# Latent attention: P times V as native fp32 matmuls instead of three fp32r matmuls on high and low parts

## The chip, the cores and the metric

The kernel runs on one core of one Trainium2 chip. A core has a matrix engine (TensorE, PE in the profile, with its weight loads shown as PEld), VectorE (DVE), ScalarE (ACT), GpSimd (POOL) and SyncE (SP), on whose queue nearly all of this kernel's DMAs are issued. The engines run their own instruction streams in order and meet at semaphores. The metric is the device time of one execution in microseconds; the times given are medians of several runs.

## The reference, cut to what matters

The kernel computes two layers of a diffusion backbone: 1024 latent tokens and 256 context tokens of width 1024. Layer 0 holds differential attention with 4 heads: each head has two query/key maps of width 64 and one value of width 128. Latent queries read all 1280 keys, context queries only the 256 context keys. Everything is in fp32.

```python
def diff_attend(q, k, v, lam):
    s = jnp.einsum('bhmqd,bhmkd->bhmqk', q, k).astype(jnp.float32) * (DA_HEAD_DIM ** -0.5)
    p = jax.nn.softmax(s, axis=-1)
    p = p[:, :, 0] - lam * p[:, :, 1]
    return jnp.einsum('bhqk,bhkv->bhqv', p.astype(v.dtype), v)
```

The last line is the product of this document. Behind it come an RMS norm over the 128 values of a head, the output projection, and a gated ConvFFN; layer 1 has pooling and retention in place of convolution and attention, and another FFN.

## The kernel before

**High and low parts.** Most matrix products are made of three fp32r matmuls: each operand x is split into a high part h, its copy in fp32r, and a low part l = x - h, and the product is h*h + h*l + l*h, accumulated in PSUM (`mm3`, lines 215 to 219). ScalarE writes the high part, VectorE subtracts for the low one. A few products, the retention in layer 1 among them (lines 1133, 1153, 1167, 1168), are given fp32 operands directly, as native fp32 matmuls.

**The stages.** Layer 0 projects all tokens, then computes the gates of the convolution, with the attention of the context tokens (`att_ctx`, line 592) and the streamed modulation matrix woven in (some 250 to 430 us of the span). Then `attention` (line 1252) weaves two generators, step by step in proportion: the context tokens' output projection and FFN (`chain`), and the attention of the latent tokens (`att_lat`, line 629). From about 860 us the latent tokens' output projection and FFN follow, then layer 1.

**A head.** `att_head` (line 658) loads K of both maps and V of one head by DMA on SP's queue. All three loads go through one buffer, `kraw`. K is cast by ScalarE and its lower half subtracted on VectorE; V is split into `vh` (line 675, ScalarE) and `vl` (line 677, VectorE), with two buffers each in the latent stage and one each in the context stage.

**A block.** `AttBlock` (line 1438) handles 512 latent queries of one head (256 for the context), as four tiles of 128 queries. For each tile, `scores` makes both maps' scores in PSUM (lines 1470 and 1471), takes the maximum on VectorE (1472) and the exponential on ScalarE (1474); there is one PSUM buffer for scores, three banks wide, so the second map waits for the first one's exponential. `combine` (line 1487, VectorE) adds the two maps with their factors. `product` transposes the combined P tile by tile of 128 keys on TensorE, four to a PSUM tile `tpp` (line 1504), copies each to `pth` (1505, ScalarE) and subtracts for `ptl` (1506, VectorE). Two query tiles share one `pth`/`ptl` pair of 256 columns; after the second one, `product` runs `mm3` for each of ten key tiles (two for the context): thirty matmuls with V as the stationary operand, into `pv`. ScalarE reads `pv` twice (1514, 1515); `stats` and `out` finish the norm and write to DRAM. There are 16 such groups of ten key tiles in the latent stage, and 4 of two in the context stage.

PSUM holds two `w` buffers, which `tpp`, `pv` and the norm's small tiles take in turn, next to the scores and three buffers of the chain. The weights of all matrix products come through one stream that runs two units ahead.

Of the kernel before, what the change touches and what calls it, by code (L numbers as in the profile page):

```python
# [9 lines left out]
F32 = mybir.dt.float32  # L10
F32R = mybir.dt.float32r
AF = mybir.ActivationFunctionType
ALU = mybir.AluOpType
# [4 lines left out]
P = 128  # L18
# [44 lines left out]
class Pool:  # L63


    def __init__(self, pool, tags):
        self.pool, self.tags = pool, tags
# [17 lines left out]
def weave(*gens):  # L85

    live = [[g, n, 0] for g, n in gens]
    while live:
        e = min(live, key=lambda e: (e[2] + 0.5) / e[1])
        if next(e[0], StopIteration) is StopIteration:  # L90
            live.remove(e)
        e[2] += 1
# [44 lines left out]
class Net:  # L137
# [454 lines left out]
    def att_ctx(self, gp, ps):  # L592

        self.att_small(gp)
        yield
        pp = Pool(ps, {"S": ("st", 1), "w": ("tp", 2)})
        ap = Pool(gp, {t: (t, 1) for t in ("kraw", "k0", "k1", "vh", "vl", "qraw", "qa0", "qa1", "qb0", "qb1", "s1", "osq",
                                          "osb", "p0", "p1", "pth", "ptl", "e1", "r1")})
        for h in range(4):
            head = self.att_head(ap, h, SEQ, CTX)  # L600
            b = AttBlock(self, ap, pp, h, SEQ, CTX, head, SEQ, CTX)
            yield
            for qt in range(2):
                b.scores(qt)
                b.combine(qt)
                yield
                b.product(qt)
                yield
            b.stats()
            yield  # L610
            b.out()
# [46 lines left out]
    def att_head(self, ap, h, t0, N):  # L658

        nc = self.nc  # L660
        K = []
        n = N // P
        for m in range(2):
            raw = ap.tile([P, N], F32, tag="kraw", name="kraw")
            for d in range(2):
                nc.sync.dma_start(raw[d * 64:(d + 1) * 64, :], self.kT[m * 64:(m + 1) * 64, h, t0:t0 + N])
            kt = ap.tile([P, N], F32R, tag=f"k{m}", name=f"k{m}")
            nc.scalar.copy(kt, raw)
            nc.vector.tensor_tensor(kt[64:128, :], raw[64:128, :], kt.bitcast(F32)[64:128, :], op=ALU.subtract)
            K.append(kt)  # L670
        raw = ap.tile([P, N], F32, tag="kraw", name="vraw")
        nc.sync.dma_start(raw.rearrange("p (t v) -> p t v", t=n),
                          self.vD[t0:t0 + N, h * P:(h + 1) * P].rearrange("(t p) v -> p t v", p=P))
        vh = ap.tile([P, N], F32R, tag="vh", name="vh")
        nc.scalar.copy(vh, raw)
        vl = ap.tile([P, N], F32R, tag="vl", name="vl")
        nc.vector.tensor_tensor(vl, raw, vh.bitcast(F32), op=ALU.subtract)
        return K, vh, vl


    def out_proj(self, xk, T, o, v, src, alloc, tmp, ps, gate):
# [570 lines left out]
    def attention(self):  # L1252

        nc, tc, I = self.nc, self.tc, self.I
        B = self.modB
        with ExitStack() as s:
            cp = s.enter_context(tc.tile_pool(name="cp", bufs=1, reuse_waits="tile"))
            ap = s.enter_context(tc.tile_pool(name="ap", bufs=1, reuse_waits="tile"))
            pp = s.enter_context(tc.tile_pool(name="psS", bufs=1, space=PSUM, reuse_waits="tile"))
            xc = cp.tile([P, 8, CTX], F32, name="xc")  # L1260
            xk = lambda k: xc[:, k, :]
            s4c = lambda: cp.tile([P, 2, CTX], F32R, tag="s4c", name="s4c", bufs=14)
            tmp = self.tmp
            ps = Pool(pp, {"mm": ("mm", 3), "tp": ("mm", 3), "st": ("mm", 3)})

            def chain():
                op = self.out_proj(xk, CTX, SEQ, 1, self.mix, s4c, tmp, ps, lambda m, v: B[:, m, v:v + 1])
                next(op)
                nc.sync.dma_start(xc, I["ctxT"])
                yield  # L1270
                yield from op
                hs = []
                yield from self.norm(xk, CTX, self.gs[(0, 2, 1)], lambda k: B[:, 8 + k, 1:2], s4c, tmp, ps, hs, True)
                big = Pool(cp, {"a": ("a", 2), "b": ("b", 1), "cv": ("cv", 2), "e": ("e", 1)})
                yield from self.ffn(0, xk, CTX, hs, 4, s4c, big, ps, lambda m: B[:, 24 + m, 1:2])
                nc.sync.dma_start(self.xcD, xc)

            at = Pool(ap, {t: (t, 2) for t in ("k0", "k1", "vh", "vl", "qa0", "qa1", "qb0", "qb1", "s1", "p0", "p1",
                                               "e1", "r1")})
            pw = Pool(pp, {"w": ("w", 2), "S": ("S", 1)})  # L1280
            ch = chain()
            for _ in range(11):
                next(ch)
            weave((ch, 9 + 2 + 22 + 6 * 4 - 11), (self.att_lat(at, pw), 68))
# [153 lines left out]
class AttBlock:  # L1438


    def __init__(self, net, ap, pp, h, q0, Q, head, k0, nk):
        nc = net.nc
        self.net, self.nc, self.ap, self.pp, self.h, self.q0, self.Q = net, nc, ap, pp, h, q0, Q
        self.K, self.vh, self.vl = head
        self.nk = nk
        self.q = []
        for m in range(2):
            raw = ap.tile([P, Q], F32, tag="qraw", name="qraw")
            for d in range(2):
                nc.sync.dma_start(raw[d * 64:(d + 1) * 64, :], net.qT[m * 64:(m + 1) * 64, h, q0:q0 + Q])  # L1450
            a = ap.tile([P, Q], F32R, tag=f"qa{m}", name=f"qa{m}")
            nc.scalar.copy(a, raw)
            b = ap.tile([P, Q], F32R, tag=f"qb{m}", name=f"qb{m}")
            nc.vector.tensor_tensor(b, raw, a.bitcast(F32), op=ALU.subtract)
            self.q.append((a, b))
        self.s1 = ap.tile([P, 4], F32, tag="s1", name="s1")
        self.sq = net.tmp.tile([P, 512], F32, tag="t2k", name="osq")[:, :Q]
        self.o = net.tmp.tile([P, 512], F32, tag="t2k", name="osb")[:, :Q]
        self.st = {}
# [32 lines left out]
    def product(self, qt):  # L1492
        nc, ap, net = self.nc, self.ap, self.net
        nkt = self.nk // P
        p = self.st.pop(qt)[0][0]
        if qt % 2 == 0:
            self.pt = [ap.tile([P, nkt, 256], F32R, tag=t, name=t) for t in ("pth", "ptl")]
        pth, ptl = self.pt
        cs = slice((qt % 2) * P, (qt % 2 + 1) * P)
        for k0 in range(0, nkt, 4):  # L1500
            n = min(4, nkt - k0)
            tp = self.pp.tile([P, 4, P], F32, tag="w", name="tpp")
            for j in range(n):
                nc.tensor.transpose(tp[:, j, :], p[:, (k0 + j) * P:(k0 + j + 1) * P], net.ident)
            nc.scalar.copy(pth[:, k0:k0 + n, cs], tp[:, :n, :])
            nc.vector.tensor_tensor(ptl[:, k0:k0 + n, cs], tp[:, :n, :], pth.bitcast(F32)[:, k0:k0 + n, cs],
                                    op=ALU.subtract)
        if qt % 2 == 1:
            pv = self.pp.tile([P, 512], F32, tag="w", name="pv")[:, :256]
            for kt in range(nkt):  # L1510
                vs = slice(kt * P, (kt + 1) * P)
                net.mm3(pv, (self.vh[:, vs], self.vl[:, vs]), (pth[:, kt, :], ptl[:, kt, :]), kt == 0, kt == nkt - 1)
            os = slice((qt - 1) * P, (qt + 1) * P)
            nc.scalar.activation(self.sq[:, os], pv, AF.Square)
            nc.scalar.mul(self.o[:, os], pv, net.subg)
# [136 lines left out]
```

## Time and profile before

| | us |
|---|---|
| median of 3 runs | 2654.31 |
| lowest, highest | 2648.61, 2654.50 |
| the profiled execution | 2658.96 |
| its span | 2657.2 |
| TensorE busy, matmuls | 2551.8 (96%) |
| TensorE busy, weight loads | 2145.4 (81%) |
| VectorE busy | 1947.5 (73%) |
| ScalarE busy | 1166.3 (44%) |
| mean granted clock of TensorE | 0.974 |

The span is what the trace covers, from the first instruction to the end of the last; the execution's time holds a little around it. Busy time is the union of an engine's instructions. Matmuls are pipelined: each record lasts longer than the time to the next one's start, so TensorE can be busy in this sense and still have room; the distance from start to start tells its pace. The granted clock is 1.00 at 2.4 GHz and 0.50 at 1.2 GHz. A tile of the program stands in a row as out<-in, with its line; "128x256" is partitions by elements.

### The profile page before, as it was taken

To read this page: it belongs to the slowest core of one execution; us is meant where nothing else is said; L and a number is where in the kernel's file an instruction comes from. 1 tells how busy PE (TensorE), PEld (TensorE's weight loads), DVE (VectorE), ACT (ScalarE), POOL (GpSimd) and SP (SyncE) were. 2 spreads that over 40 slices of the span, in tenths; PEclk is the share of its full clock that TensorE was granted. 3 is DMA by queue.
4 is the path that set the end of the run, shared out by engine and by line. 5 is a ranking of instruction groups with operands and counts; after the bars stand their busy time and mean duration, and the time that the engine had idled before them with its cause. 6 is when DMAs were issued, how large, how long until landed. Compare 5 with 4: busy or idle time off the path is not lost.

```text
span 2657.2 us, 34664 instructions
## 1 busy us (share of the span) xinstructions
PE 2551.8 (96%) x12666; PEld 2145.4 (81%) x12666; DVE 1947.5 (73%) x3077; ACT 1166.3 (44%) x1751; POOL 241.4 (9%) x321
## 2 busy tenths in 40 slices
PE   6999998999998998999999998999899999999999
PEld 6777887999997886888888886877688788888887
DVE  7467965999997587777778978446558766666984
ACT  5322324767675354444443454133235444444442
POOL 3221000000000041000000002013203100000000
PEclk6999999999999999999999999999799999999999
DMA  7224545443433624434458664577662222225874
GB/s 257 93 95 135 182 135 165 134 143 112 124 116 111 232 65 149 134 127 133 130 178 302 218 206 141 177 232 222 191 217 72 103 88 80 87 80 202 281 242 139
DMA packets 209547, 414.01 MB, mean 156 GB/s; under 512 B 20320, under 2 KB 89568, under 8 KB 208992
## 3 DMA queue, kind: packets, MB, share of 16 engines
q1 hardware_dynamic: 206352, 406.41, 46.6%
q10 hardware_dynamic: 3024, 5.38, 0.6%
q8 instruction: 99, 1.62, 0.3%
q14 instruction: 72, 0.59, 0.1%
HBM read 341.98 MB, written 69.73 MB: 155 GB/s over the span
## 4 chain that ended last, share of the span: by engine, by line
PE 63%; DVE 13%; issue 12%; DMA 7%; ACT 3%; POOL 2%; SPq 0%; ACTq 0%; DVEq 0%; POOLq 0%
PE PA L217 4%; PE PA L218 4%; PE PA L219 4%; PE pd L218 3%; PE pd L219 3%; PE pd L217 3%; PE PB L217 2%; PE PB L218 2%; PE PB L219 2%; PE pt L217 2%; PE pt L218 2%; PE pt L219 2%; PE po L218 2%; PE po L217 2%; PE po L219 2%
## 5 line engine op out<-in xcount | busy, mean ns | idle before, releaser
L114 DVE TENSOR_TENSOR wl<-wr,wh 128x1024 fp32r<-128x1024 f32 x254 | 309.6, 1221 | 178.4 <-ACT wh L112 176.1
L112 ACT CAST wh<-wr 128x1024 fp32r<-128x1024 f32 x254 | 261.9, 1034 | 394.1 <-PE PA L218 67.3
L217 PE MATMUL pd<-s,wh 128*128 128x512 f32 x616 | 241.2, 392 | 4.9 <-ACT s L963 4.9
L218 PE MATMUL pd<-s,wh 128*128 128x512 f32 x616 | 241.4, 392 | 1.8 <-DVE s L964 1.8
L219 PE MATMUL pd<-s,wl 128*128 128x512 f32 x616 | 241.1, 391 | 0.0
L217 PE MATMUL PA<-s,wh 128*128 128x512 f32 x544 | 212.2, 390 | 0.2 <-DVE a L893 0.2
L219 PE MATMUL PA<-s,wl 128*128 128x512 f32 x544 | 211.8, 389 | 0.0
L218 PE MATMUL PA<-s,wh 128*128 128x512 f32 x544 | 211.8, 389 | 0.0
L351 DVE SCALAR_TENSOR_TENSOR mw<-mw,cr 128x256 f32<-128x256 f32 x256 | 111.4, 458 | 81.3 <-DMA mw<-in_mod1T 71.9
L112 ACT CAST wh<-r 128x1024 fp32r<-128x1024 f32 x80 | 67.0, 837 | 220.6 <-PE PB L218 126.5
L217 PEld LDWEIGHTS pd<-s,wh 128*128 128x128 f32 x616 | 116.4, 189 | 29.4 <-ACT s L963 5.3
L218 PEld LDWEIGHTS pd<-s,wh 128*128 128x128 f32 x616 | 116.4, 189 | 27.2 <-DVE s L964 3.2
L219 PEld LDWEIGHTS pd<-s,wl 128*128 128x128 f32 x616 | 116.4, 189 | 24.2
L217 PE MATMUL PB<-s,wh 128*128 128x512 f32 x320 | 125.0, 390 | 1.2 <-ACT p L889 1.2
L218 PE MATMUL PB<-s,wh 128*128 128x512 f32 x320 | 124.8, 390 | 0.0
L219 PE MATMUL PB<-s,wl 128*128 128x512 f32 x320 | 124.6, 389 | 0.0
L217 PEld LDWEIGHTS PA<-s,wh 128*128 128x128 f32 x544 | 102.2, 188 | 22.3 <-DVE a L893 1.3
L219 PEld LDWEIGHTS PA<-s,wl 128*128 128x128 f32 x544 | 102.1, 188 | 21.2
L218 PEld LDWEIGHTS PA<-s,wh 128*128 128x128 f32 x544 | 102.2, 188 | 21.1
L1474 ACT ACTIVATE p<-S,s 128x1280 f32<-128x1280 f32 (+1 forms) x80 | 92.9, 1161 | 52.7 <-DVE s L1472 51.2
L359 POOL TENSOR_TENSOR rr<-vv,mhalf 128x8 f32<-128x8 f32 (+2 forms) x39 | 57.6, 1478 | 587.8 <-DVE vv L357 563.3
L1472 DVE TENSOR_REDUCE s<-S 128x1 f32<-128x1280 f32 (+1 forms) x80 | 102.0, 1275 | 11.1 <-PE S L1471 10.1
(385 smaller groups left out, 7000.3 us busy)
## 6 DMA issues: line engine op xcount, KB each, us to landing
wr<-in_w_up SPq DMA_DIRECT2D x98, 512.0 KB, 3.4
wr<-in_w_dn SPq DMA_DIRECT2D x92, 512.0 KB, 4.3
gr<-gD SPq DMA_DIRECT2D x154, 256.0 KB, 3.7
mw<-in_mod1T SPq DMA_DIRECT2D x256, 128.0 KB, 3.2
gD<-fcv SPq DMA_DIRECT2D x44, 512.0 KB, 3.6
wr<-in_w_out SPq DMA_DIRECT2D x40, 512.0 KB, 4.2
r<-in_w_up SPq DMA_DIRECT2D x40, 512.0 KB, 3.3
mbw<-in_mod0T SPq DMA_DIRECT2D x32, 512.0 KB, 3.6
```

Of the source, the lines that this page charges most:

```text
L112: self.nc.scalar.copy(hi, raw)
L114: eng.tensor_tensor(lo, raw, hi.bitcast(F32), op=ALU.subtract)
L217: mm(out, L[0], R[0], start=first, stop=False)
L218: mm(out, L[0], R[1], start=False, stop=False)
L219: self.last_mm = mm(out, L[1], R[0], start=False, stop=last)
L351: self.nc.vector.scalar_tensor_tensor(w, in0=w, scalar=1.0, in1=c, op0=ALU.mult, op1=ALU.mult, accum_out=d)
L359: self.last_pow = nc.gpsimd.tensor_tensor(r, vv, self.mhalf[:, :n], op=ALU.pow)
L1472: nc.vector.tensor_reduce(s2[:, m:m + 1], sv, axis=AX.X, op=ALU.max, negate=True)
L1474: nc.scalar.activation(e, sv, AF.Exp, bias=s2[:, m:m + 1], accum_out=self.s1[:, qt:qt + 1] if m == 0 else s2[:, 2:3])
```

## The change

`product` writes the transposed P once, as fp32, into `pt`, and multiplies it with V as it came from DRAM, one native fp32 matmul per key tile. The high copies and low subtractions of P and V go, V gets a buffer of its own in place of `kraw` (two in the latent stage, one in the context stage), and `pt` has two buffers in the latent stage where `pth` and `ptl` had one each. Scores, softmax and everything else stay. The product's arithmetic becomes that of the fp32 matmul instead of the three-term sum.

```diff
@@ -594,8 +594,8 @@
         self.att_small(gp)
         yield
         pp = Pool(ps, {"S": ("st", 1), "w": ("tp", 2)})
-        ap = Pool(gp, {t: (t, 1) for t in ("kraw", "k0", "k1", "vh", "vl", "qraw", "qa0", "qa1", "qb0", "qb1", "s1", "osq",
-                                          "osb", "p0", "p1", "pth", "ptl", "e1", "r1")})
+        ap = Pool(gp, {t: (t, 1) for t in ("kraw", "k0", "k1", "vh", "qraw", "qa0", "qa1", "qb0", "qb1", "s1", "osq",
+                                          "osb", "p0", "p1", "pt", "e1", "r1")})
         for h in range(4):
             head = self.att_head(ap, h, SEQ, CTX)
             b = AttBlock(self, ap, pp, h, SEQ, CTX, head, SEQ, CTX)
@@ -668,14 +668,10 @@
             nc.scalar.copy(kt, raw)
             nc.vector.tensor_tensor(kt[64:128, :], raw[64:128, :], kt.bitcast(F32)[64:128, :], op=ALU.subtract)
             K.append(kt)
-        raw = ap.tile([P, N], F32, tag="kraw", name="vraw")
-        nc.sync.dma_start(raw.rearrange("p (t v) -> p t v", t=n),
+        V = ap.tile([P, N], F32, tag="vh", name="V")
+        nc.sync.dma_start(V.rearrange("p (t v) -> p t v", t=n),
                           self.vD[t0:t0 + N, h * P:(h + 1) * P].rearrange("(t p) v -> p t v", p=P))
-        vh = ap.tile([P, N], F32R, tag="vh", name="vh")
-        nc.scalar.copy(vh, raw)
-        vl = ap.tile([P, N], F32R, tag="vl", name="vl")
-        nc.vector.tensor_tensor(vl, raw, vh.bitcast(F32), op=ALU.subtract)
-        return K, vh, vl
+        return K, V
 
 
     def out_proj(self, xk, T, o, v, src, alloc, tmp, ps, gate):
@@ -1275,7 +1271,7 @@
                 yield from self.ffn(0, xk, CTX, hs, 4, s4c, big, ps, lambda m: B[:, 24 + m, 1:2])
                 nc.sync.dma_start(self.xcD, xc)
 
-            at = Pool(ap, {t: (t, 2) for t in ("k0", "k1", "vh", "vl", "qa0", "qa1", "qb0", "qb1", "s1", "p0", "p1",
+            at = Pool(ap, {t: (t, 2) for t in ("k0", "k1", "vh", "pt", "qa0", "qa1", "qb0", "qb1", "s1", "p0", "p1",
                                                "e1", "r1")})
             pw = Pool(pp, {"w": ("w", 2), "S": ("S", 1)})
             ch = chain()
@@ -1441,7 +1437,7 @@
     def __init__(self, net, ap, pp, h, q0, Q, head, k0, nk):
         nc = net.nc
         self.net, self.nc, self.ap, self.pp, self.h, self.q0, self.Q = net, nc, ap, pp, h, q0, Q
-        self.K, self.vh, self.vl = head
+        self.K, self.V = head
         self.nk = nk
         self.q = []
         for m in range(2):
@@ -1494,22 +1490,20 @@
         nkt = self.nk // P
         p = self.st.pop(qt)[0][0]
         if qt % 2 == 0:
-            self.pt = [ap.tile([P, nkt, 256], F32R, tag=t, name=t) for t in ("pth", "ptl")]
-        pth, ptl = self.pt
+            self.pt = ap.tile([P, nkt, 256], F32, tag="pt", name="pT")
+        pt = self.pt
         cs = slice((qt % 2) * P, (qt % 2 + 1) * P)
         for k0 in range(0, nkt, 4):
             n = min(4, nkt - k0)
             tp = self.pp.tile([P, 4, P], F32, tag="w", name="tpp")
             for j in range(n):
                 nc.tensor.transpose(tp[:, j, :], p[:, (k0 + j) * P:(k0 + j + 1) * P], net.ident)
-            nc.scalar.copy(pth[:, k0:k0 + n, cs], tp[:, :n, :])
-            nc.vector.tensor_tensor(ptl[:, k0:k0 + n, cs], tp[:, :n, :], pth.bitcast(F32)[:, k0:k0 + n, cs],
-                                    op=ALU.subtract)
+            nc.scalar.copy(pt[:, k0:k0 + n, cs], tp[:, :n, :])
         if qt % 2 == 1:
             pv = self.pp.tile([P, 512], F32, tag="w", name="pv")[:, :256]
             for kt in range(nkt):
                 vs = slice(kt * P, (kt + 1) * P)
-                net.mm3(pv, (self.vh[:, vs], self.vl[:, vs]), (pth[:, kt, :], ptl[:, kt, :]), kt == 0, kt == nkt - 1)
+                net.last_mm = nc.tensor.matmul(pv, self.V[:, vs], pt[:, kt, :], start=kt == 0, stop=kt == nkt - 1)
             os = slice((qt - 1) * P, (qt + 1) * P)
             nc.scalar.activation(self.sq[:, os], pv, AF.Square)
             nc.scalar.mul(self.o[:, os], pv, net.subg)
```

## Rows read from the trace of the kernel before

**Rows 1.** Stretch, length; busy PE, PEld, DVE, ACT, POOL; clock; DMA share, GB/s.

```profile
480.00:825.00 345.00, 340.30 (x2607) 323.70 (x2605) 325.56 (x475) 241.04 (x417) 15.08 (x47) 1.00 0.40 123
822.00:860.00 38.00, 27.58 (x181) 24.96 (x180) 27.05 (x45) 18.82 (x34) 1.01 (x1) 0.90 0.32 112
```

**Rows 2.** Timeline of TensorE in latent attention (start, length, instruction).

```profile
506.99 0.28 PE L217 MATMUL pv<-pth,vh 128*128 128x256 f32 x1
...
510.41 0.39 PE L1471 MATMUL S<-k,qb 128*128 128x512 f32 x1
510.64 0.28 PE L1470 MATMUL S<-k,qa 128*128 128x256 f32 x1
...
510.87 0.28 PE L219 MATMUL pab<-s4c,wl 128*128 128x256 f32 x1
...
511.94 0.28 PE L219 MATMUL pab<-s4c,wl 128*128 128x256 f32 x1
...
841.27 1.03 PE L1504 MATMUL tpp<-ident,p 128*128 128x128 f32 x8
```

**Rows 3.** TensorE's instructions by form, 480 to 825 (busy, mean ns, idle).

```profile
L219 PE MATMUL pab<-s4c,wl 128*128 128x256 f32 x327 | 93.9, 287 | 0.0
...
L1470 PE MATMUL S<-k,qa 128*128 128x512 f32 x115 | 48.4, 421 | 1.8 <-ACT p L1474 1.4
...
L217 PE MATMUL pd<-s4c,wh 128*128 128x256 f32 x163 | 46.8, 288 | 0.0
...
L1504 PE MATMUL tpp<-ident,p 128*128 128x128 f32 x288 | 42.6, 274 | 1.0 <-DVE osb L1533 0.5 <-DVE ptl L1506 0.4
...
L217 PE MATMUL pv<-pth,vh 128*128 128x256 f32 x140 | 39.4, 281 | 0.1
```

**Rows 4.** Timeline of all engines at the start of latent attention.

```profile
459.36 0.63 PE L375 MATMUL rb<-ident,rr 128*128 128x128 f32 x2
...
460.38 1.49 DVE L677 TENSOR_TENSOR vl<-vraw,vh 128x1280 fp32r<-128x1280 f32 x1 [2.11 <-ACT vh L675]
...
461.79 0.47 DVE L402 SCALAR_TENSOR_TENSOR nt<-xc,gs,rb 128x256 f32<-128x256 f32 x1
```

**Rows 5.** What TensorE waited for, 822 to 860 us (total us, times, longest).

```profile
PE S L1470 <- ACT p L1474: 3.7, 2, 2.8
PE tpp L1504 <- DVE p L1487: 2.3, 1, 2.3
...
PE tpp L1504 <- DVE ptl L1506: 1.4, 1, 1.4
```

**Rows 6.** Timeline of TensorE in the retention stage: native fp32 matmuls.

```profile
1822.67 1.13 PE L1153 MATMUL at<-q,kTt 64*128 64x256 f32 x4
...
1828.42 1.03 PE L1167 MATMUL o<-am,V 128*128 128x256 f32 x4
1829.28 0.60 PE L1168 MATMUL o<-qd,St 128*128 128x256 f32 x2
```

**Rows 7.** The same columns as rows 1, for two stretches of retention.

```profile
1822.50:1830.00 7.50, 7.49 (x42) 5.46 (x41) 7.13 (x22) 2.27 (x4) 0.17 (x3) 1.00 0.66 196
1889.00:1904.00 15.00, 13.41 (x28) 8.39 (x29) 10.52 (x26) 0.60 (x1) 3.20 (x3) 0.54 0.57 184
```

**Rows 8.** VectorE's low parts of P by form, 250 to 860 us.

```profile
L1506 DVE TENSOR_TENSOR ptl<-tpp,pth 128x512 fp32r<-128x512 f32 x64 | 42.4, 684 | 0.6 <-ACT pth L1505 0.5
L1506 DVE TENSOR_TENSOR ptl<-tpp,pth 128x256 fp32r<-128x256 f32 x40 | 16.8, 420 | 2.7 <-ACT pth L1505 2.2
```

**Rows 9.** Timeline of TensorE: first and last matmul of the last group.

```profile
850.29 0.58 PE L217 MATMUL pv<-pth,vh 128*128 128x256 f32 x1
...
856.17 0.28 PE L219 MATMUL pv<-pth,vl 128*128 128x256 f32 x1
```

**Rows 10.** Timeline of SP and TensorE in the context heads.

```profile
309.98 0.38 SPq L672 DMA_DIRECT2D vraw<-vD  x1
...
312.65 0.28 PE L219 MATMUL pv<-pth,vl 128*128 128x256 f32 x1
```

## The prediction, made before the changed kernel ran

> **What bounds the kernel now.** I read three views, in this order: the busy time of each engine over the stretch of latent attention, the instructions of TensorE in that stretch by form, and its timeline there. The reader is to see first that two engines look full at once [rows 1]: over the 345 us from 480 to 825 us TensorE's matmuls show 340.3 us busy and VectorE 325.6 us. A matmul's record carries its latency, so records overlap, and the busy time cannot say how much room TensorE has. Its pitch can. From the timeline [rows 2]: thirty matmuls of P times V start between 506.99 and 510.41 us, 0.114 us each; a score matmul of 512 columns takes 0.23 us from start to start (510.41 to 510.64); nine FFN matmuls of 256 columns take 1.07 us (510.87 to 511.94), 0.119 us each; eight transposes, in a row of 1.03 us that ends with one matmul of 0.274 us, start every 0.108 us. Now the counts [rows 3]: three lines of 327 and three of 163 FFN matmuls, 1470 x 0.119 = 174.9 us; two lines of 115 score matmuls of 512 columns, 52.9 us, and half as many of 256 at half the pitch, 13.2 us; 288 transposes, 31.1 us; three lines of 140 for P times V, 47.9 us. That is 320 us of 345, and the small column sums and broadcasts are not in it. So TensorE is the bound of this stretch, with at most some 25 us not accounted for and only 345 - 340.3 = 4.7 us in which no matmul is under way at all. VectorE is nearly as full, but it rarely makes TensorE wait here.
>
> Before and after that stretch it is different. At its start TensorE stands idle for an operand of the context FFN [rows 4], and in the last 38 us, from 822 to 860, it is busy for only 27.6 us [rows 1], waiting for the exponentials, for the combination of the two softmax maps and for the low part of P [rows 5].
>
> **Part by part: the matmuls.** The change replaces three fp32r matmuls per tile of 128 keys by one fp32 matmul. The retention stage runs native fp32 matmuls of exactly this shape, 128 rows and columns against 256 columns, and shows each as two records [rows 6]: four records (two matmuls of line 1167) start between 1828.42 and 1829.28 us, 0.215 us each, and within the group (1.03 - 0.38)/3 = 0.217, where 0.38 is a record's own length, read from two in 0.60 us, one pitch of 0.217 before the last record. I take 0.216, so one matmul costs 0.432 us against 3 x 0.114 = 0.342. A latent group of ten key tiles goes from 3.42 to 4.32 us, and there are 16 of them: +14.4 us. A context group has two key tiles, +0.18 us, four times: +0.7. The sum is +15.1 us, all on the engine that is the bound. By the rows a record is 0.216/0.114 = 1.9 pitches of an fp32r matmul, and there are two. The Trainium skill, "FP8 and Floating Point Precision", section TensorE Precision Notes, says that true FP32 takes four passes through the array. Counting passes alone, four for three, would give 168 x 0.114 = 19.2 us, 4 us more than these rows; I keep the rows, since they carry the pitch itself.
>
> What entering native fp32 from fp32r costs the trace only bounds: the 64-row matmuls that follow fp32r in the retention stage take 1.13 us for four records where the 128-row ones take 1.03 [rows 6], so up to 0.1 us for each of 16 groups, 1.6 us. Below nothing it can't go, since no pass is saved. I take nothing, because the group of 128 rows, the nearest in shape, shows no such excess.
>
> **Part by part: VectorE and ScalarE.** The low part of P goes: 64 subtractions of 0.684 us and 40 of 0.420 us [rows 8], and the four latent low parts of V, 1.49 us each by the one of the first head [rows 4]: 42.4 + 16.8 + 6.0 = 65 us of VectorE. ScalarE loses eight casts of V and keeps all copies of P's transposes. Where TensorE is the bound this is worth only what TensorE now waits for. In the long stretch that is at most the 4.7 us of idle time, and at least nothing; I take 3, as most of it comes behind the exponentials, which wait for VectorE's maxima, and VectorE falls from 94% to about 78% there (14 of 16 groups, so 7/8 of the 65 us).
>
> At the start [rows 4] the broadcast of the context norm is done at 459.36 + 0.63 = 459.99 us, but the first VectorE step that reads it starts at 461.79, behind the subtraction of V, for which VectorE's queue had stood 2.11 us until ScalarE's cast of V was there. Cast and subtraction go: 461.79 - 459.99 = 1.8 us back, between nothing and 4 us (if those 2.11 us count too).
>
> At the end [rows 5]: the 1.4 us that the last transposes wait for the low part go entirely. Of the 3.7 us behind exponentials and the 2.3 us behind the combination, both queued in VectorE among these subtractions, I take half, 3.0; so 4.4 us, between nothing and 7.4. Against it stands the last group of P times V, which ran at the lower clock: 30 matmuls started from 850.29 to 856.17 us [rows 9], 0.20 us each where 0.114 is the full pitch. Twenty fp32 records at twice 0.216 (an estimate from the retention's records [rows 6] and the two levels) would take 8.6 us, 2.7 more than now, of which 0.9 is counted above: +1.8 if the clock falls there again, nothing if the shorter wait keeps it up. I take 1.8.
>
> In the context heads, woven into the gates, VectorE loses eight subtractions of P and four of V, some 12 x 0.42 = 5 us; the bounds are 0 and 5, and I take 1, as TensorE is close to full there as well.
>
> **Part by part: the DMA of V.** V is now loaded straight into its own buffer and no longer shares one with the two K loads, so it needn't wait for K's subtraction. It waits instead for the matmuls of the head that last used the buffer, on SP's queue, with query loads and weight loads behind it. In the latent stage there are two buffers, and the head two before is done. In the context stage there is one: the third head's load was issued at 309.98 us, and the group before ended after 312.65 [rows 10], so it would hold SP's queue some 3 us; likewise for the fourth head. I cost it at nothing: the weight stream runs two units ahead, and one unit feeds 72 matmuls. If that cover is gone, it is 3 us twice.
>
> **Sum.** 15.1 - 3 - 1.8 - 4.4 + 1.8 - 1 = +6.7 us. The profiled execution took 2658.96 us (span 2657.2), so 2665.7 for its like; the median of the runs shown is 2654.31, 4.65 us below it, and the forecast by that is 2661.0 us.
>
> **Rivals.** Slower: TensorE is bound throughout and little of VectorE's time comes back. The place is the stretch from 480 to 825 us; its price is the 15.1 us with the entry cost of 1.6 and the clock's 1.8, less at most half of what I return, so +13 to +18.5 us, about 2670. It decides as soon as less than 8.9 of the 10.2 us that I return come back with the clock's 1.8 paid, so whenever I have been slightly generous; for it speaks that waits on the low part of P are a few us in all, against it the 10 us of idle TensorE in the tail. Dearer, and rare: the native matmuls let the clock fall in every group. From 1822.5 to 1830 us TensorE ran nothing but fp32 matmuls and transposes for 7 us and the granted clock stayed at 1.00; from 1889 to 1904 the same kinds of matmul were dense at a mean clock of 0.54 after a wait [rows 7]. So a fallen clock is slow to come back, but a dense group doesn't lose it. At half the clock 16 groups would cost 16 x 4.3 = 69 us more: 2730.
>
> Faster: VectorE is what sets the pace. For it speaks its 94%. All the idle time of the three places, 4.7 + 4 + 7.4, and 5 us in the context heads against 15.1 give -6.0 us, 2648; it needs a tighter order of matmuls besides to pass 0.3%, as in part of the 25 us above: 2640. There is also the busy share of TensorE's weight loads: 323.7 us of 345, no more than VectorE's [rows 1]. If that were TensorE's true measure, the change would lighten it too: 14 groups lose ten of the stretch's 2605 loads each, at 323.7/2605 = 0.124 us (an estimate) 17 us, and with room on both engines the stretch might shrink by as much, to about 2637. The Trainium skill, "Perfetto Trace Analysis", section Identifying the Most-Contended Engine, does judge TensorE's room by its weight loads rather than by its matmuls' busy time. The rows' pitches speak against it: the native records are twice as long, so the loads thin out while the array stays full.
>
> That the change doesn't do what it says has no room here: the shape and type of the new matmul stand in the retention rows.
>
> **How the numbers follow.** This kernel's measurement can tell about 0.3% from no change, 8 us: 2646.3 to 2662.3. My forecast, +6.7 us with bounds from -6 to +8, has 0.47; the slower rival 0.36; the fallen clock 0.03; the faster rival 0.14. So faster 0.14, within 0.3% 0.47, slower 0.39. The bounds of the unknown costs run from 15.1 - 4.7 - 4 - 7.4 - 5 = -6.0 to 15.1 + 1.6 + 1.8 = +18.5, that is 2648 to 2673; with two us for the spread of the runs on either side, 2646 to 2675, which leaves out the fallen clock and most of the faster rival.
>
> **What would show it.** P times V as 20 records per latent group at 0.216 us, 336 records in all; no subtraction at lines 1506 and 677; VectorE near 78% from 480 to 825 while TensorE stays full and the stretch is some 10 us longer; the start and the last 38 us shorter by 2 to 5 us each; the clock at 1.00 through the groups. I am wrong if the native records come at another pitch, if the stretch doesn't grow, or if the clock falls inside it.

## The result, and where the time went

The changed kernel took 2675.01 us (median of four runs, 2670.6 to 2679.1) against 2654.25 us before: a ratio of 1.0083, with an interval from 1.0062 to 1.0104, or 20.8 us. Two further comparisons, each with runs of the kernel before on the same chip, gave 1.0071 (1.0057 to 1.0086; 19.4 us) and 1.0071 (1.0058 to 1.0085; 17.9 us). So the change costs 18 to 21 us, where I had forecast 6.7 and "within 0.3%".

The changed matmul came out as predicted. Its form in the stretch from 480 to 825 us of the kernel after (busy, mean ns, idle before):

```profile
L1506 PE MATMUL pv<-pT,V 128*128 128x256 f32 x270 | 62.4, 382 | 0.0
```

And one group on TensorE's timeline there (start, length, instruction):

```profile
507.76 4.48 PE L1506 MATMUL pv<-pT,V 128*128 128x256 f32 x20
```

Twenty records end 4.48 us after the first one starts. With 0.38 us for the last record's own length that is (4.48 - 0.38)/19 = 0.216 us each, the pitch of the retention's native matmuls [rows 6]; a group takes 4.3 us where it took 3.4 [rows 2].

Then the engines, with the columns of rows 1: the same 345 us, and the last 38 us of the stage, which lie 17 us later now.

```profile
480.00:825.00 345.00, 340.32 (x2359) 313.91 (x2358) 271.05 (x371) 226.59 (x398) 8.60 (x46) 1.00 0.36 114
839.00:877.00 38.00, 30.86 (x179) 25.75 (x177) 24.57 (x36) 21.04 (x38) 1.01 (x1) 0.95 0.43 145
```

VectorE fell from 325.6 us to 271.1, 94% to 79%, and TensorE shows 340.3 us busy as before [rows 1]: 54 us of VectorE's work left the stretch and none of TensorE's 4.7 us of idle time came back. What TensorE waited for, first in the kernel before from 480 to 825 us, then in the kernel after from 480 to 842 us (total us, times, longest):

```profile
PE S L1470 <- ACT p L1474: 1.4, 3, 1.0
PE orb L375 <- POOL r L1527: 0.9, 1, 0.9
PE tpp L1504 <- DVE osb L1533: 0.5, 1, 0.5
PE tpp L1504 <- DVE ptl L1506: 0.4, 2, 0.2
```

```profile
PE S L1466 <- ACT p L1470: 2.5, 2, 1.5
PE tpp L1500 <- ACT pT L1501: 1.8, 1, 1.8
```

And from 839 to 877 us:

```profile
PE tpp L1500 <- DVE p L1483: 4.3, 1, 4.3
PE orb L375 <- POOL r L1521: 1.4, 1, 1.4
PE S L1466 <- ACT p L1470: 0.8, 1, 0.8
```

Only 0.9 us of the old waits in the long stretch were for VectorE itself, and only 0.4 us for the low part. In the kernel after, a wait of the transposes for ScalarE's copy of P is new there. In the tail the wait for the low part is gone [rows 5], but the wait for the combination of the maps is 4.3 us instead of 2.3: between the last scores and that wait TensorE has 17 FFN matmuls left, where it had 10 transposes and 20 FFN matmuls before.

**Where the 18 us are.** I cut the stage at four instructions: the last matmul of the context gates (tile pb), the first FFN matmul of the stage (pab), the last score matmul (S) and the last broadcast of the attention's norm (orb). Every kernel of this study is listed with its profiles, in us from start to start; the experiments are told below.

| kernel (profiles) | A: pb to pab | B: pab to last S | C: S to last orb | A + B + C |
|---|---|---|---|---|
| before (2) | 43.4, 41.9 | 373.9, 375.4 | 18.5, 18.3 | 435.7 |
| after (3) | 47.7, 45.2, 44.3 | 388.8, 391.7, 389.6 | 17.0, 18.2, 18.2 | 453.6 |
| after, subtractions kept (2) | 43.4, 43.2 | 388.6, 387.2 | 19.2, 20.4 | 451.0 |
| after, V late (2) | 39.7, 39.4 | 391.3, 389.7 | 17.0, 17.0 | 447.1 |
| before, no low parts (2) | 43.1, 40.0 | 376.3, 374.9 | 15.2, 15.5 | 432.5 |
| before, V early (1) | 44.4 | 380.5 | 18.5 | 443.4 |
| after, every native matmul twice (1) | 47.0 | 451.1 | 21.7 | 519.8 |
| before, one fp32r matmul (1) | 41.9 | 359.1 | 14.3 | 415.3 |

(The last column is the mean.) Before against after: +3.1 at the start, +15.4 in the body, -0.6 in the tail, together +17.9. Up to the last pb matmul the two are level (423.9 and 423.5 us before; 422.6, 424.1 and 425.6 after). The two ends of A in the first profile of the changed kernel, and below them in the second one with V late (durations, then first and last start; the pb rows hold what lies between 415 and 430 us, the pab rows between 460 and 475):

```profile
L219 PE MATMUL pb<-h,wl x12: 388/389/389, 415.1 to 422.6; 128*128 128x512 f32 x12
L217 PE MATMUL pab<-s4c,wh x7: 278/415/415, 470.3 to 474.9; 128*128 128x256 f32 x7
```

```profile
L219 PE MATMUL pb<-h,wl x16: 388/389/389, 416.2 to 426.4; 128*128 128x512 f32 x16
L217 PE MATMUL pab<-s4c,wh x16: 282/401/562, 465.8 to 474.9; 128*128 128x256 f32 x16
```

The cut between B and C does not part the same work in every kernel. In B the kernel before has 300 transposes and 508 of the FFN's pd matmuls, the changed kernel 310 and 511, the one with the subtractions kept 310 and 521. At 0.108 and 0.119 us [rows 2], some 1.4 us of work have only changed sides between before and after, and 1.2 us between the changed kernel and the one with the subtractions. B + C, from pab to orb, is free of that: 393.0 us before, 407.8 after, 407.7 with the subtractions kept, 407.5 with V late, 391.0 without low parts.

**The start got longer, not shorter.** SP's queue (start, time that the issue took, line, transfer) and ScalarE's casts of weights there, of the kernel after:

```profile
437.83 0.43 SPq L672 DMA_DIRECT2D V<-vD  x1
440.50 0.45 SPq L666 DMA_DIRECT2D kraw<-kT  x1
441.76 0.33 SPq L106 DMA_DIRECT2D wr<-in_w_up  x1
442.14 0.45 SPq L666 DMA_DIRECT2D kraw<-kT  x1
...
445.06 8.82 SPq L106 DMA_DIRECT2D wr<-in_w_up  x2
...
451.22 1.04 ACT L112 CAST wh<-wr 128x1024 fp32r<-128x1024 f32 x1 [4.61 <-DMA wr<-in_w_up]
```

V's 640 KB go out at 437.83, ahead of the second map of K and of an FFN weight tile. The weight tile issued at 441.76 is cast at 451.22, 9.5 us later, after ScalarE stood 4.6 us for it; VectorE's part follows, the weight buffer comes free, and only then does the second of the two loads at 445.06 leave SP's queue, at 453.88. The kernel before has V behind the subtraction of K, at 452.71, and the same weight tile takes 7.0 us:

```profile
441.54 0.33 SPq L106 DMA_DIRECT2D wr<-in_w_up  x1
...
448.52 1.05 ACT L112 CAST wh<-wr 128x1024 fp32r<-128x1024 f32 x1 [0.82 <-DMA wr<-in_w_up]
...
452.71 0.38 SPq L672 DMA_DIRECT2D vraw<-vD  x1
```

The broadcast that I had counted on is late with all this. The kernel after, all engines:

```profile
463.10 0.69 PE L375 MATMUL rb<-ident,rr 128*128 128x128 f32 x2 [1.03 <-POOL rr L359]
463.82 0.87 DVE L402 SCALAR_TENSOR_TENSOR nt<-xc,gs,rb 128x256 f32<-128x256 f32 x2 [0.47 <-PE rb L375]
```

The first step that reads it starts 0.03 us after its end, so the 1.8 us that it stood behind the subtraction of V [rows 4] are indeed gone. But the broadcast starts at 463.10 instead of 459.36.

### The profile page after: what moved, and what is told of

The parts are those of the page before. It is cut to its first block, busy times and chain, and to the rows that moved or that the text cites. A ratio compares the mean times of both kernels' runs of the same rounds, so it can differ in the third digit from the quotient of the medians.

```text
span 2672.5 us, 34222 instructions
## 1 busy us (share of the span) xinstructions
PE 2567.6 (96%) x12498; PEld 2150.3 (80%) x12498; DVE 1896.9 (71%) x2965; ACT 1158.9 (43%) x1743; POOL 237.1 (9%) x321
## 4 chain that ended last, share of the span: by engine, by line
PE 62%; DVE 14%; issue 13%; DMA 7%; ACT 3%; POOL 2%; SPq 0%; ACTq 0%; DVEq 0%; POOLq 0%
PE PA L217 4%; PE PA L218 4%; PE PA L219 4%; PE pd L218 3%; PE pd L219 3%; PE pd L217 3%; PE pv L1506 3%; PE PB L217 2%; PE PB L218 2%; PE PB L219 2%; PE pt L217 2%; PE pt L218 2%; PE pt L219 2%; PE po L218 2%; PE po L217 2%
```

## The experiments

Theory: TensorE is the bound of the stage and the dearer matmul goes into the time in full; VectorE's relief returns next to nothing; the load of V, freed from the buffer that it shared with K, goes out early and delays the start. Rivals: the relief did give back what I had predicted, and the matmuls cost more; the longer start has another cause.

**Subtractions of P kept for nobody.**

```diff
             self.pt = ap.tile([P, nkt, 256], F32, tag="pt", name="pT")
+            self.ptl = ap.tile([P, nkt, 256], F32R, tag="ptl", name="ptl", bufs=1)
 ...
             nc.scalar.copy(pt[:, k0:k0 + n, cs], tp[:, :n, :])
+            nc.vector.tensor_tensor(self.ptl[:, k0:k0 + n, cs], tp[:, :n, :], pt[:, k0:k0 + n, cs], op=ALU.subtract)
```

> The changed kernel with VectorE's subtraction for the low part of P put back, into a buffer that no matmul reads (104 more subtractions, 64 of about 0.68 us and 40 of about 0.42 us, 59 us of VectorE in all); P times V stays native fp32. It takes back only the relief of VectorE. Theory (TensorE is the bound of latent attention and the relief returned next to nothing there, 0 to 3 us): the time of the changed kernel plus 0 to 4 us, 2675 to 2679. Rival (the relief did return some 6 to 10 us, and the native matmuls cost more than 15 us): 2681 to 2686.

Measured 2667.01 us, 1.0063 times the kernel before of that chip (2648.48). That is 8 us below what I had expected, of which 5.8 us are the chip, by the two medians of the kernel before. It was run again beside the changed kernel on one chip:

> The changed kernel a third time, so that it stands on one chip beside the next three. Theory: 17 to 21 us over the kernel before, with the stretch from the last context gate matmul to the first FFN matmul of the stage at 45 to 48 us and the stage behind it at 405 to 410 us. Rival (the stretch's length is an execution's own): that stretch at 42 to 44 us.

> The changed kernel with VectorE's subtraction for the low part of P put back for nobody, a second time, beside the changed kernel on the same chip. Theory (the relief of VectorE returned nothing that a timing can tell): within 3 us of the changed kernel, either way. Rival (it returned the 9 us that the prediction gave back): 6 to 10 us slower than the changed kernel. Second rival (without the subtractions the order of work gets worse): 3 us or more faster than the changed kernel.

The changed kernel gave 2667.65 (1.0071 times before), this one 2670.01 (1.0072): the same. VectorE stood at 312.7 of 345 us again, TensorE at 341.4 (second profile, columns of rows 1):

```profile
480.00:825.00 345.00, 341.44 (x2392) 318.84 (x2391) 312.70 (x461) 226.32 (x397) 11.28 (x45) 1.00 0.35 112
```

So 59 us of VectorE's work, taken away or put back, move the time by nothing that shows. By the table C is 2.0 us shorter without it (17.8 against 19.8) and B 2.1 us longer, so B + C stays the same. The changed kernel's A was 44.3 us there, between what I had set for the theory and for the rival; this kernel's was 43.2.

**The relief alone.** The kernel before, with the high parts in the place of the low ones:

```diff
-        vl = ap.tile([P, N], F32R, tag="vl", name="vl")
-        nc.vector.tensor_tensor(vl, raw, vh.bitcast(F32), op=ALU.subtract)
-        return K, vh, vl
+        return K, vh, vh
 ...
-            self.pt = [ap.tile([P, nkt, 256], F32R, tag=t, name=t) for t in ("pth", "ptl")]
-        pth, ptl = self.pt
+            self.pt = ap.tile([P, nkt, 256], F32R, tag="pth", name="pth")
+        pth = ptl = self.pt
```

and without the subtraction for `ptl`.

> The kernel before without the low parts: no subtraction for P and none for V, the high parts stand in their places, and P times V is still three fp32r matmuls per key tile (the low parts' share of the product is left out). It has the relief of VectorE (65 us of work gone) without the dearer matmuls, and V still goes through the buffer that it shares with K. Theory (TensorE bound): 0 to 5 us faster than before, 2649 to 2654, most of it at the start of latent attention and in the tail. Rival (VectorE had set the pace as well): 10 us faster or more, 2644 or less.

> The kernel before without the low parts of P and V, three fp32r matmuls per key tile of high parts only, a second time: the first gave 5 us over before by the medians although its profile's attention stage was 1 us shorter. Theory (the relief returns nothing; the rest is the scatter of executions behind the stage): within 4 us of the kernel before, its attention stage again at 391 to 393 us. Rival (the relief makes the stage longer): 4 us or more slower, the stage at 395 us or more.

Measured 2653.73 and 2651.14 us, 1.0012 (0.9999 to 1.0025) and 1.0007 (0.9997 to 1.0018) times before: no gain, where the theory had up to 5 us and the rival more than 10. The stage is 391.5 and 390.4 us from pab to orb (B + C) against 392.3 and 393.7, so it did not get longer: C is 3.1 us shorter, B 1 us longer (it holds ten transposes more), in all 2 us less. The medians can't show so little, since executions of one kernel spread over 10 us and more (last section).

**V late.** The changed kernel, V's load of the latent heads kept behind the last query load of the head's first block:

```diff
+        def load():
+            nc.sync.dma_start(V.rearrange("p (t v) -> p t v", t=n), ...)
 ...
+        if late:
+            with net.tc.issue_after(dq.ins):
+                late.pop()()
```

> The changed kernel with the load of V of each latent head issued behind the last query load of that head's first block, as it came in the kernel before, where V shared K's staging buffer. Theory (in the changed kernel V's load, free of that buffer, went ahead of K map 1's halves and of the FFN weights and lengthened the hole at the start of latent attention by some 4 us): 3 to 5 us faster than the changed kernel, 2670 to 2672, and the broadcast of the context norm is read within a microsecond of the end of the low half of the first FFN weights. Rival (the longer hole has another cause, such as the order in which the planner places work there): the same as the changed kernel within 1.5 us.

> The changed kernel with the load of V of each latent head behind the query loads of its first block, a second time, beside the changed kernel on the same chip. Theory (the early load of V costs the start of latent attention its hole): 4 to 8 us faster than the changed kernel, that stretch at 39 to 41 us. Rival (the first time it was the chip): within 2 us of the changed kernel.

Measured 2663.11 us (1.0052) and 2664.10 us (1.0055), the second 3.6 us below the changed kernel on the same chip, a little less than the 4 to 8 us that I had set. A is 39.7 and 39.4 us, 6.2 us less than the changed kernel's mean of 45.7 and 3.1 less than before; B + C is the same as in the changed kernel, so the early loads of the later heads cost nothing that shows. The second profile's timeline, as above:

```profile
444.07 0.33 SPq L106 DMA_DIRECT2D wr<-in_w_up  x1
...
449.16 1.05 ACT L112 CAST wh<-wr 128x1024 fp32r<-128x1024 f32 x1
449.29 0.59 SPq L674 DMA_DIRECT2D V<-vD  x1
449.92 1.90 SPq L106 DMA_DIRECT2D wr<-in_w_up  x2
...
459.55 0.69 PE L375 MATMUL rb<-ident,rr 128*128 128x128 f32 x2 [1.95 <-POOL rr L359]
460.28 0.87 DVE L402 SCALAR_TENSOR_TENSOR nt<-xc,gs,rb 128x256 f32<-128x256 f32 x2 [1.34 <-PE rb L375]
```

The weight tile is cast 5.1 us after its issue, the next two leave SP within 1.9 us instead of 8.8, and the broadcast comes 33.1 us after the last pb matmul (at 426.4) instead of 40.5, 37.2 and 36.9 in the three profiles of the changed kernel. With V out of the way the return at the start that I had predicted is there in full, and more.

**V early in the kernel before.** Its staging buffer taken from the second softmax map instead of K's:

```diff
-        raw = ap.tile([P, N], F32, tag="kraw", name="vraw")
+        raw = ap.tile([P, N], F32, tag="p1" if N == TOT else "kraw", name="vraw")
```

> The kernel before with one thing changed: V's staging buffer in the latent heads is not the one that K's halves use but that of the second softmax map, which is free then, so that V's load needn't wait for K's subtraction and is issued early. High and low parts and the three matmuls stay. Theory (the early load of V collides with the loads of K map 1 and of the FFN weights): 2 to 5 us slower than before, 2656 to 2659, with the landings of K map 1 and of the first weights stretched by 2 to 4 us at the start of latent attention. Rival (an early V does no harm): the same as before or up to 2 us faster.

Measured 2659.64 us, 1.0035 times before (1.0022 to 1.0049): 11 us slower, more than either side expected. At the start the theory's part is there: V at 435.10, the weight tile cast 8.3 us after its issue, A 44.4 us. But most of the loss, some 6 us, is in the body, where two waits of the norm's broadcast for GpSimd make 2.9 us between 620 and 700 us. The buffer that V borrows is one of two that the second map's exponentials need in every query tile, so this kernel doesn't tell the early load alone, and what the body lost to it is left open.

Over all fourteen profiles the time from the issue of that weight tile to its cast is 5.1 to 7.0 us where V comes behind it (seven profiles, mean 5.9) and 7.0 to 9.5 us where V goes ahead (seven, mean 8.1). The effect of V's order on that tile is clear; within each kind some 2 us are an execution's own, and so the first profile of the changed kernel shows more of it than the other two. A as a whole parts the two kinds less sharply: 39.4 to 43.4 us with V behind, 43.2 to 47.7 with V ahead. The kernel with the subtractions kept has V ahead too, and its A is 43.3 us, 2.4 less than the changed kernel's; why is open. So the price of V's order lies between 3.6 us (the medians) and 6.2 us (the profiles of the pair in which nothing else differs).

**The price of the matmuls, up.** Each native matmul twice:

```diff
-                net.last_mm = nc.tensor.matmul(pv, self.V[:, vs], pt[:, kt, :], start=kt == 0, stop=kt == nkt - 1)
+                nc.tensor.matmul(pv, self.V[:, vs], pt[:, kt, :], start=kt == 0, stop=False)
+                net.last_mm = nc.tensor.matmul(pv, self.V[:, vs], pt[:, kt, :], start=False, stop=kt == nkt - 1)
```

> The changed kernel with each native matmul of P times V issued twice into the same accumulator (so the product is doubled, which the norm behind it takes out but for its epsilon): 168 matmuls of two records of 0.216 us more, 72.6 us of TensorE. Theory (TensorE is the bound, each added pitch goes into the time one for one): 68 to 74 us slower than the changed kernel, TensorE's pitch in the groups still 0.216 us. Rival (TensorE has slack behind VectorE and ScalarE, so a part is hidden): less than 60 us.

It ran on one chip with the changed kernel and a second profile of the kernel before:

> The changed kernel as it is, a second time, beside the kernel before on the same chip as the runs of this call. It shows how much of the 20.8 us between the two medians is the change and how much the spread of executions. Theory (native matmuls +15, start of latent attention 0 to +4 from V's early load, tail -2): +14 to +18 us over the kernel before. Rival (the start's +4.4 us of the first profile is the change's own and not an execution's): +19 us or more, and the stretch from the last context gate matmul to the first FFN matmul of the stage again near 47.7 us, where the kernel before shows 43.4 and the kernel with the subtraction put back showed 43.4 as well.

> The kernel before, a second profile. Theory: the stretch from the last context gate matmul to the first FFN matmul is 43 us again, and from there to the last matmul of the stage's last norm 392 us; if the profile is shorter than the first one, the difference lies behind 1880 us, where the two first profiles stood at the lower clock for some 7 us longer than the four experiments. Rival (the attention stage itself differs from execution to execution): those two stretches come out 3 us or more apart from the first profile.

The changed kernel took 2676.27 us (2656.86 before): its 19.4 us are a little over the rival's border, while its A of 45.2 us lies about halfway between the two kernels' first profiles. With each matmul twice it was 2733.81 us: +57.5 us, under the 60 us that I had set as the rival's border, which would speak for hidden time. The profiles say otherwise: the stage is 66.2 us longer than the changed kernel's mean, for 160 matmuls of 0.432 us = 69.1 us in it, so 96% of the price; the pairs still start every 0.43 us (511.54 to 511.97), and TensorE has almost no gap (timeline, then 420 us of the stage with the columns of rows 1):

```profile
511.54 0.59 PE L1506 MATMUL pv<-pT,V 128*128 128x256 f32 x2
511.97 0.59 PE L1507 MATMUL pv<-pT,V 128*128 128x256 f32 x2
```

```profile
480.00:900.00 420.00, 418.27 (x2770) 385.19 (x2768) 283.46 (x385) 236.49 (x411) 11.63 (x47) 1.00 0.31 96
```

What the medians lack is not in the stage, as far as the profiled executions tell: from its end to the end of the run the changed kernel's profile on this chip took 1796 us, this kernel's 1789, with the same code. The second profile of the kernel before repeated the stage (A 41.9, B + C 393.7 us). It is 2.9 us shorter than the first, most of it behind 1900 us, but not in the stretch that I had named, which was as long again.

**The price of the matmuls, down.** The kernel of the relief alone, with one matmul of the high parts:

```diff
-                net.mm3(pv, (self.vh[:, vs], self.vl[:, vs]), (pth[:, kt, :], ptl[:, kt, :]), kt == 0, kt == nkt - 1)
+                net.last_mm = nc.tensor.matmul(pv, self.vh[:, vs], pth[:, kt, :], start=kt == 0, stop=kt == nkt - 1)
```

> The kernel of the relief alone (no low parts) with one fp32r matmul per key tile in place of three, so the product of the high parts alone: 336 matmuls of 0.114 us fewer, 38.3 us of TensorE. Theory (TensorE is the bound; VectorE at some 80% follows): 30 to 38 us faster than the kernel before. Rival (VectorE or ScalarE comes up at once as the next bound): 10 to 20 us faster.

Measured 2630.66 us, 0.9909 times before (0.9890 to 0.9928): 26 us faster, between the two. In the stage, 320 matmuls x 0.114 = 36.5 us less of TensorE gave 17.2 us against the relief alone, not quite half (and 20.4 us against the kernel before; the rest of the 26 lies outside the stage). What TensorE waits for from 480 to 880 us now:

```profile
PE S L1468 <- ACT p L1472: 7.3, 5, 2.8
PE tpp L1502 <- DVE p L1485: 5.6, 2, 5.2
PE pd L219 <- DVE wl L114: 4.8, 2, 3.5
```

So, by one profile in each direction, the stage is bound by TensorE upward almost one for one, and downward for about half of what I took away; then the exponentials, the combination and the weights' low parts come up together. This is the only kernel here that beats the one before, and it does so by leaving out two of the three terms of the product.

## Why the prediction was wrong, step by step

**The matmuls, +15.1: right.** Two pairs of kernels that differ in little but the matmul (and in V's load) give the price in the stage: subtractions kept against before, 451.0 - 435.7 = 15.3 us; V late against the relief alone, 447.1 - 432.5 = 14.6. From pab to orb alone they give 14.7 and 16.5. The sum had 14.4 for the latent groups, and I had taken no entry cost; the runs leave room for some 2 us, with it for the second buffer of `pt`, which no run tests by itself. The Trainium skill, "FP8 and Floating Point Precision", section TensorE Precision Notes, counts four passes for true FP32. By an estimate from that count the latent groups would cost 160 x 0.114 = 18.2 us, more than any of these sums, so the pitch of the rows decides.

**VectorE's relief in the long stretch, -3: failed, it is nothing.** The reasoning was that most of the 4.7 us of idle time came behind the exponentials and so behind VectorE. But the waits of the kernel before have 1.4 us behind the exponentials, and only 0.4 us behind the low part. VectorE's share fell to 79%, and TensorE's idle time stayed at 4.7 us: it now waits for ScalarE's exponentials and copies. Both pairs that test it (after against subtractions kept, relief against before) have B longer by 2.1 and 1.0 us with the relief. The change as a whole says the same: from pab to orb my terms were 14.4 - 3 - 4.4 + 1.8 = 8.8 us, and it grew by 14.8, the matmuls' 14.4 with nothing returned.

**The start, -1.8: the mechanism right, the sum of the place wrong.** The queueing behind V's subtraction went, as the row of nt shows, and with V late A falls by 3.1 us, within my bounds of 0 to 4. In the changed kernel A grew by 3.1.

**The load of V, costed at nothing: this failed too, by as much as the relief.** I looked only for a wait that the load might add to SP's queue, in the context heads. There I was right: the third head's load sits 1.53 us in the queue instead of 3, the fourth's 0.43, and that part of the run isn't longer. What I did not ask is what a load does that no longer waits. The buffer shared with K had kept V out of the way of the K map and the weights which the start of the stage needs first; taken out, it went 15 us earlier, ahead of them, and A went from 39.6 (V late) to 45.7 us. That is 6.2 us, 3.6 by the medians, in a term that had no bounds in my range. That the result passed the upper end of that range, 2675, is chance: it did so by 0.01 us, and the 19.4 and 17.9 us of the other two comparisons, added to 2654.3, would have stayed inside. That it came 11 to 14 us above the forecast of +6.7 is not: in the profiles the relief that did not come makes 6.0 us of it (from pab to orb) and the start 4.9.

**The tail, -4.4 and +1.8: both failed, in opposite directions.** In the pairs the relief makes C 2.0 to 3.1 us shorter, but B gets longer by 2.1 and 1.0, so that from pab to orb it returns nothing with the native matmuls and 2 us with the fp32r ones. The clock's price did not come: the twenty records of the last group started over 5.2, 5.7 and 5.8 us in the three profiles, not over 8 and more, and the thirty of before over 5.9 and 5.7 [rows 9]. Only a part of the group stands at the lower clock now. The first profile's last group on TensorE's timeline, and the clock there (columns of rows 1):

```profile
867.70 5.54 PE L1506 MATMUL pv<-pT,V 128*128 128x256 f32 x20
```

```profile
866.00:870.00 4.00, 3.94 (x15) 2.83 (x14) 0.63 (x1) 1.54 (x3) 0.00 (x0) 0.57 0.75 255
870.00:875.00 5.00, 4.18 (x23) 3.62 (x22) 0.16 (x1) 1.73 (x4) 0.34 (x1) 1.00 0.03 9
```

C comes to -0.6 us in all, where my terms gave -2.6 besides the group's 0.9, and some 1.4 us of its work now stand in B.

**The context heads, -1 and +0.7:** nothing to see; the last pb matmul starts within some 2 us of where it did, either way.

**The rivals.** The one that I gave 0.36 was right in its mechanism: TensorE bound throughout and little returned, +13 to +18.5 us. With V late, that is without the load that it did not reckon with either, the change costs 14.6 and 14.3 us by the medians; that the changed kernel itself, at 17.9 to 20.8, comes near its upper end is the load of V, and so luck. Its border (it decides once less than 8.9 of 10.2 us come back) was so close that I should have seen it as the likelier: the rows showed VectorE's low parts as the last wait for 1.4 us in the tail [rows 5] and 1.8 us at the start [rows 4], and the rest of what I returned was not shown to hang on them. The fallen clock is refuted: 1.00 from 480 to 842 us. So is VectorE as the pace. The Trainium skill, "Perfetto Trace Analysis", section Identifying the Most-Contended Engine, judges TensorE's room by the busy share of its weight loads, beside the work done against the peak. The weight loads fell from 323.7 to 313.9 us in the stretch while the body grew by 15 us, so here the matmuls' pitch was the measure.

## What to carry to other kernels

Where one engine is bound by the pitch of its matmuls, price the change by the pitch and give back nothing for work that another engine loses, unless a wait for that very work ends last; here some 60 us of VectorE were worth nothing with the native matmuls and 2 us with the fp32r ones. When a change takes a shared buffer away, ask which transfer it had held back, and what now stands behind that one in the queue: an accidental wait can be a good order, and it can be had back by an explicit one (V late: 3.6 us by the medians). A bound that holds one for one upward can end soon downward: here 36.5 us less of TensorE's work, 8% of the stage, brought half.

## What the runs showed of the hardware

A load that goes ahead stretches those behind it: with V's 640 KB in front, 512 KB of weights took 8.1 us on average from issue to cast, with V behind 5.9 us.

The same code behind the stage took 1787 to 1798 us in the profiles of this study, although nothing there was changed. One place of it is the end of the retention stage, 33.5 to 33.9 us in three profiles and 26.9 to 28.0 in eleven (from the last kv matmul to the last at matmul). The granted clock is lower in a long one, 0.90 over 30 us where a short one has 1.00. The same columns, of the changed kernel's first profile and then of its second one:

```profile
1880.00:1910.00 30.00, 27.65 (x122) 21.12 (x122) 16.90 (x56) 5.18 (x8) 7.60 (x8) 0.90 0.62 194
```

```profile
1885.00:1915.00 30.00, 28.48 (x134) 21.90 (x135) 18.01 (x59) 6.35 (x10) 8.95 (x9) 1.00 0.66 202
```

Why it differs from one execution to the next stayed open. For a change of some microseconds in one stage, the profiles of that stage repeated to 3 us, in one kernel to 4, while whole executions of one kernel spread over 10 us and more.
